# Down products of two feed-forward layers: seven block products in place of eight

## The chip, the core and the metric

The kernel runs on one core of one Trainium2 chip. The metric is the device time of one execution in microseconds (us). Matmuls run on TensorE (PE in the rows below, PEld for its weight loads), elementwise work on VectorE (DVE), ScalarE (ACT) and GpSimd (POOL); SyncE (SP) issues nearly all DMA transfers.

## The reference

Two transformer blocks over 1024 tokens of width 1024, in float32. Three feed-forward layers are in them, each with a hidden width of 2816 = 22 tiles of 128. The first has a convolution behind its up product; the second and third, which the change touches, are

```python
def swiglu(x, w_gu, w_down):
    g, u = jnp.split(x @ w_gu, 2, axis=-1)
    return (jax.nn.silu(g) * u) @ w_down

f = swiglu(rms_norm_2(h, ffn1_pre_g[i]), ffn1_w_gu[i], ffn1_w_down[i])
h = h + 0.5 * rms_norm_2(f, ffn1_post_g[i])
```

The order in the whole program: modulation, mixers and attention of block 1; feed-forward layer 1; layer 2; attention of block 2; layer 3; a gated embedding at the end.

## The kernel before

Every float32 operand of a matmul is split into a high and a low part (`Core.split`, lines 56 to 59: ACT copies the high part at line 58, DVE subtracts it at line 59), and each product is three matmuls: high by high, high by low, low by high. All matmuls of interest are 128 x 128 by 128 x 512.

`ffn` (line 189 on) has two stages.

**Up product.** Hidden tiles 0 and 1 are made plainly (lines 248 to 252). For tiles 2 to 21 the loop at line 323 makes gate and value together by seven block products (B11, T4, B21, T1, T2, B22, T3; `prod`, line 293: 12 matmuls each, 84 for one tile). `weights(j)` (line 271) loads the weights of one tile into `raw` buffers, makes differences on POOL and splits them. `finish_tile` (line 301) makes the gated hidden tile `s` and writes it to the DRAM tensor `hidden` (line 320). One pass of the loop takes five buffers of tag `b4`: T and t4 (lines 276 and 287), X (326), s and V (331).

**Down product.** `yacc` holds the eight output tiles of 128 tokens in SBUF. `load(j)` (line 355) brings back hidden tile j and the same 128 rows of `w_down` and splits both. `down` (line 366) takes a pair of hidden tiles and adds its product to `yacc`: for each of 8 token tiles and 2 column halves, 2 x 3 matmuls into one PSUM bank, then one add by DVE (line 377; ACT copies for the first pair, line 375). That is nine pairs of 96 matmuls, and at the end one call with four tiles (192 matmuls), between which the next norm is begun (`finish`).

Buffers: `b4` 12 of 4 KB per partition, `raw` 3, `wh` and `wl` 4 each, `hh` and `hl` 2 each of 16 KB (they hold the transposed input of the up product), PSUM `mm` 6 banks and `tp` 2. The tile framework decides the order on each engine: by the order of the program, but what is ready may go ahead of an earlier line that is not. A buffer is free again when all that reads it is done.

Of the kernel before, what the change touches and what calls it, by code (L numbers as in the profile page):

```python
# [5 lines left out]
F32 = mybir.dt.float32  # L6
F32R = mybir.dt.float32r
I32 = mybir.dt.int32
AF = mybir.ActivationFunctionType
OP = mybir.AluOpType  # L10
PSUM = bass.MemoryType.PSUM
DRAM = bass.MemoryType.DRAM
P = 128
D = 1024
# [174 lines left out]
def ffn(k, hT, w_gu, w_down, nff, prep, finish, taps=None, then=None):  # L189
# [2 lines left out]

    nc, v, pool = k.nc, k.nc.vector, k.nc.gpsimd
    with k.tc.tile_pool(name="ffn", bufs=1) as fp:
        k.places(fp, "b4", 12)
        hidden = k.dr.tile([nff, P, D], F32, name=f"hidden{k.count()}")

        def b4(dt=F32):  # L200
            return fp.tile([P, D], dt, name="b4", tag="b4", bufs=12)

        def big(shape, dt):
            return fp.tile([P] + shape, dt, name="S", tag="S", bufs=3)
# [54 lines left out]
        for a in range(0, 4, 2):  # L259
            c = slice(a, a + 2)  # L260
# [10 lines left out]
        def weights(j):  # L271

            rg, rv = k.raw([P, 8, P]), k.raw([P, 8, P])
            nc.sync.dma_start(rg, w_gu[:, j * P:j * P + P].rearrange("(k p) n -> p k n", p=P))
            nc.sync.dma_start(rv, w_gu[:, (j + nff) * P:(j + nff) * P + P].rearrange("(k p) n -> p k n", p=P))
            T = b4().rearrange("p (k n) -> p k n", k=8)
            pool.tensor_tensor(T[:, up], rv[:, up], rg[:, up], op=OP.subtract)
            W1 = [w.rearrange("p (k n) -> p k n", k=8) for w in k.wide()]
            k.split(*W1, rg)
            pool.tensor_tensor(T[:, dn], rv[:, dn], T[:, up], op=OP.subtract)  # L280
            pool.tensor_tensor(rv[:, up], rv[:, dn], rv[:, up], op=OP.subtract)
            W2 = [w.rearrange("p (k n) -> p k n", k=8) for w in k.wide()]
            k.split(*W2, T)
            W3 = [w.rearrange("p (k n) -> p k n", k=8) for w in k.wide()]
            k.split(*W3, rv)
            pool.tensor_tensor(T[:, up], rg[:, dn], T[:, dn], op=OP.subtract)  # L286
            t4 = b4(F32R).rearrange("p (a k n) -> p a k n", a=2, k=4)
            k.split(t4[:, 0], t4[:, 1], T[:, up])
            both = lambda W, c: (W[0][:, c], W[1][:, c])
            return dict(B11=both(W1, up), B21=both(W1, dn), T1=both(W2, up), T2=both(W2, dn), T3=both(W3, up),  # L290
                        B22=both(W3, dn), T4=(t4[:, 0], t4[:, 1]))

        def prod(ps, w, x, start):
            for a in range(4):
                for n, (y, z) in enumerate(((0, 0), (0, 1), (1, 0))):
                    nc.tensor.matmul(ps, w[y][:, a], x[z][:, a], start=start and a == 0 and n == 0, stop=a == 3 and n == 2,  # L296
                                     skip_group_check=True)

        lo, hi = slice(0, 512), slice(512, 1024)

        def finish_tile(j, A, w, s, V):

            prod(A, w["T4"], A22, False)
            if taps is None:
                nc.scalar.activation(s[:, hi], A, AF.Silu)
                v.tensor_tensor(s[:, hi], s[:, hi], V[:, hi], op=OP.mult)
            else:
                nc.scalar.activation(s[:, hi], A, AF.Copy)
                us = []
                for m, z in ((j, s), (j + nff, V)):  # L310
                    u = b4()
                    t = [taps[:, a, m:m + 1] for a in range(4)]
                    nc.scalar.activation(u, z, AF.Identity, bias=t[3], scale=t[1])
                    v.scalar_tensor_tensor(u[:, 1:], z[:, :D - 1], t[0], u[:, 1:], op0=OP.mult, op1=OP.add)
                    v.scalar_tensor_tensor(u[:, :D - 1], z[:, 1:], t[2], u[:, :D - 1], op0=OP.mult, op1=OP.add)
                    us.append(u)
                s = us[0]
                nc.scalar.activation(s, s, AF.Gelu_apprx_tanh)
                v.tensor_tensor(s, s, us[1], op=OP.mult)
            nc.sync.dma_start(hidden[j], s)  # L320

        prev = None
        for j in range(2, nff):
            w = weights(j)
            A, B, C = k.mm(), None, None
            X = b4()
            prod(A, w["B11"], A11, True)
            nc.scalar.activation(X[:, lo], A, AF.Copy)  # L328
            if prev is not None:
                finish_tile(*prev)  # L330
            s, V = b4(), b4()
            B = k.mm()
            prod(B, w["B21"], A12, True)
            v.tensor_tensor(s[:, lo], B, X[:, lo], op=OP.add)
            if taps is None:
                nc.scalar.activation(s[:, lo], s[:, lo], AF.Silu)
            C = k.mm()
            prod(C, w["T1"], S1, True)
            nc.scalar.activation(X[:, hi], C, AF.Copy)
            prod(A, w["T2"], S2, False)  # L340
            nc.scalar.activation(X[:, lo], A, AF.Copy)
            prod(C, w["B22"], S4, False)
            v.tensor_tensor(V[:, lo], C, X[:, lo], op=OP.add)  # L343
            if taps is None:
                v.tensor_tensor(s[:, lo], s[:, lo], V[:, lo], op=OP.mult)
            prod(A, w["T3"], S3, False)
            v.tensor_tensor(V[:, hi], A, X[:, hi], op=OP.add)
            prev = (j, A, w, s, V)
        finish_tile(*prev)


        ys = [big([4, D], F32) for _ in range(2)]
        yacc = [ys[i // 4][:, i % 4] for i in range(NT)]

        def load(j):
            r = k.raw([P, D])
            nc.sync.dma_start(r, hidden[j])
            h = b4(F32R), b4(F32R)
            k.split(*h, r)
            r = k.raw([P, D])  # L360
            nc.sync.dma_start(r, w_down[j * P:(j + 1) * P, :])
            w = k.wide()
            k.split(*w, r)
            return h + w

        def down(ready, first, last):
            for i in range(NT):
                t = slice(i * P, i * P + P)
                for n in range(2):
                    c = slice(n * 512, n * 512 + 512)  # L370
                    po = k.mm()
                    for a, (hh, hl, wh, wl) in enumerate(ready):
                        k.mm3(po, (hh[:, t], hl[:, t]), (wh[:, c], wl[:, c]), a == 0, a == len(ready) - 1)
                    if first:
                        nc.scalar.activation(yacc[i][:, c], po, AF.Copy)
                    else:
                        v.tensor_tensor(yacc[i][:, c], yacc[i][:, c], po, op=OP.add)  # L377
                if last:
                    finish(fp, i, yacc[i])
                    if i >= 4:  # L380
                        k.flush(2, 1)

        n = nff - 4
        for j in range(0, n, 2):
            down([load(j), load(j + 1)], j == 0, False)
        rows = big([4, D], F32)
        k.rows = [rows[:, a] for a in range(3)]
        k.junk = rows[:, 3]
        prep(fp)
        down([load(j) for j in range(n, nff)], False, True)  # L390
        k.close()
        if then is not None:
            then(fp)
# [10 lines left out]
class Filler:  # L404
# [21 lines left out]
    def finish(self, gen=None):  # L426
        while self.jobs and (gen is None or gen in self.jobs):
            self.step()
# [1299 lines left out]
def body(tc, ctx, p, out):  # L1728
# [80 lines left out]
    rows = []  # L1809
    fin, nxt2 = step(2, rows)  # L1810
    ffn(k, nxt[0], p["w_up"], p["w_down"], 22, loader(rows, (m[3], 1.0), (p["ffn1_pre_g_2"], 1.0)), fin, taps=taps)
    rows = []
    fin, nxt3 = step(3, rows)
    ffn(k, nxt2[0], p["ffn1_w_gu_2"], p["ffn1_w_down_2"], 22, loader(rows, (p["ffn1_post_g_2"], 0.5), (p["attn_pre_g_2"], 1.0)), fin)
    e = [k.dr.tile([P, D], F32, name=f"e{i}") for i in range(NT)]
    mT = attention2(k, nxt3[0], p["w_in_2"], p["b_in_2"], tabA, tabB, p["sinks_2"],
# [10 lines left out]
    def last(pool):  # L1827
        ple(k, pool, nxt5[0], e, p["w_ple_gate_2"], loader(rows6, (p["ple_post_g_2"], 1.0)), fin6)

    ffn(k, nxt4[0], p["ffn2_w_gu_2"], p["ffn2_w_down_2"], 22, loader(rows, (p["ffn2_post_g_2"], 0.5), (p["ple_pre_g_2"], 1.0)), fin,  # L1830
        then=last)

# [36 lines left out]
```

## Time and profile before

| | us |
|---|---|
| median of 3 runs | 3281.38 |
| lowest, highest | 3278.68, 3285.41 |
| the profiled execution | 3276.33 |
| its span, first to last instruction | 3274.3 |

The profile is that of one execution. The busy time of an engine is the time in which it runs instructions; matmuls overlap in their pipeline, so their mean duration is longer than the distance from one to the next. "Idle before" names what the engine waited for.

### The profile page before, as it was taken

How to read it: one execution, taken by the hardware profiler on the slowest of the kernel's cores; microseconds unless marked ns; L12 is line 12 of the kernel's file. 1: busy time of each engine (PE TensorE's matmuls, PEld its weight loads, DVE VectorE, ACT ScalarE, POOL GpSimd, SP SyncE). 2: the span in 40 equal slices, each digit the busy share in tenths (PEclk: the TensorE clock that was granted, in tenths of full speed). 3: DMA queues.
4: the chain of work that ended last, by engine and by line, in shares of the span. 5: the costliest groups of instructions: out<-in, count | busy, mean ns of one | idle time of the engine just before them, and what ended most of it. 6: DMA issues, size and time to landing. Idle time of an engine off the chain costs nothing. (4 is left out here: it accounts for less than half of the span.)

```text
span 3274.3 us, 40844 instructions
## 1 busy us (share of the span) xinstructions
PE 3088.8 (94%) x15362; PEld 2523.1 (77%) x15362; DVE 2133.0 (65%) x3648; ACT 1274.7 (39%) x1975; POOL 788.9 (24%) x903
## 2 busy tenths in 40 slices
PE   5989988899999998999999999999998999999988
PEld 2766767788887878888888878777787788888867
DVE  7766588766666678444446686667677444456686
ACT  3335633444543124333341145446623333341132
POOL 3468525322220014322300020000014222200022
PEclk8999999999999999999999999999998999999999
DMA  7573553122224232222242342111631222242344
GB/s 207 172 223 118 159 175 118 65 90 78 84 90 142 92 129 71 89 78 86 88 141 92 96 142 82 46 45 68 212 129 52 84 77 90 84 148 94 98 144 154
DMA packets 282104, 362.87 MB, mean 111 GB/s; under 512 B 35559, under 2 KB 208871, under 8 KB 281906
## 3 DMA queue, kind: packets, MB, share of 16 engines
q1 hardware_dynamic: 273442, 345.73, 32.7%
q10 hardware_dynamic: 6576, 9.00, 0.8%
q0 software_dynamic: 1888, 5.53, 0.6%
q8 instruction: 121, 1.98, 0.2%
q14 instruction: 77, 0.63, 0.1%
HBM read 274.84 MB, written 91.66 MB: 112 GB/s over the span
## 5 line engine op out<-in xcount | busy, mean ns | idle before, releaser
L296 PE MATMUL mm<-S,wh 128*128 128x512 f32 x1440 | 443.5, 389 | 2.0 <-ACT b L328 2.0
L96 PE MATMUL mm<-wh,b 128*128 128x512 f32 x1056 | 414.3, 393 | 4.0 <-ACT b L58 4.0
L97 PE MATMUL mm<-wl,b 128*128 128x512 f32 x1056 | 413.4, 392 | 0.0
L98 PE MATMUL mm<-wh,b 128*128 128x512 f32 x1056 | 411.9, 391 | 0.0
L377 DVE TENSOR_TENSOR S<-S,mm 128x512 f32<-128x512 f32 x432 | 289.1, 684 | 128.9 <-PE mm L98 128.0
L59 DVE TENSOR_TENSOR wl<-raw,wh 128x1024 fp32r<-128x1024 f32 x242 | 320.3, 1325 | 60.6 <-ACT wh L58 60.4
L58 ACT ACTIVATE wh<-raw 128x1024 fp32r<-128x1024 f32 x244 | 253.4, 1053 | 261.7 <-PE mm L296 140.2
L296 PEld LDWEIGHTS mm<-S,wh 128*128 128x128 f32 x1440 | 270.2, 188 | 58.6 <-ACT b L328 2.4
L96 PE MATMUL mm<-hh,wh 128*128 128x256 f32 (+1 forms) x880 | 300.1, 341 | 15.5 <-ACT hh L58 15.3
L97 PE MATMUL mm<-hl,wh 128*128 128x256 f32 (+1 forms) x880 | 298.9, 340 | 3.5 <-DVE hl L59 3.5
L98 PE MATMUL mm<-hh,wl 128*128 128x256 f32 (+1 forms) x880 | 297.0, 338 | 4.6 <-DVE wl L59 4.6
L296 PE MATMUL mm<-hh,wh 128*128 128x512 f32 x720 | 284.0, 395 | 13.6 <-ACT wh L58 9.8
L296 PE MATMUL mm<-hh,wl 128*128 128x512 f32 x720 | 283.5, 394 | 9.8 <-DVE wl L59 9.8
L296 PE MATMUL mm<-hl,wh 128*128 128x512 f32 x720 | 283.1, 393 | 0.0
L296 PE MATMUL mm<-S,wl 128*128 128x512 f32 x720 | 280.2, 389 | 0.0
L151 POOL TENSOR_TENSOR S<-S 128x1024 f32<-128x1024 f32 x24 | 58.9, 2453 | 802.6 <-ACT S L145 785.9
L343 DVE TENSOR_TENSOR b<-mm,b 128x512 f32<-128x512 f32 x60 | 41.5, 692 | 319.4 <-PE mm L296 314.1
L96 PEld LDWEIGHTS mm<-wh,b 128*128 128x128 f32 x1056 | 199.9, 189 | 45.6 <-ACT b L58 4.5
L97 PEld LDWEIGHTS mm<-wl,b 128*128 128x128 f32 x1056 | 200.0, 189 | 42.5 <-DVE wl L59 0.9
L98 PEld LDWEIGHTS mm<-wh,b 128*128 128x128 f32 x1056 | 199.2, 189 | 42.7 <-DVE b L59 1.2
L58 ACT ACTIVATE b<-raw 128x1024 fp32r<-128x1024 f32 x66 | 69.6, 1059 | 402.1 <-PE mm L97 247.6
L286 POOL TENSOR_TENSOR b<-raw,b 128x512 f32<-128x512 f32 x60 | 79.7, 1329 | 573.8 <-DVE wl L59 573.8
(385 smaller groups left out, 6454.0 us busy)
## 6 DMA issues: line engine op xcount, KB each, us to landing
raw<-in_ffn_w_gu SPq DMA_DIRECT2D x88, 512.0 KB, 3.8
hidden<-b SPq DMA_DIRECT2D x66, 512.0 KB, 2.6
raw<-hidden SPq DMA_DIRECT2D x66, 512.0 KB, 4.5
raw<-in_w_ada SPq DMA_DIRECT2D x48, 512.0 KB, 3.7
raw<-in_w_up SPq DMA_DIRECT2D x44, 512.0 KB, 3.8
raw<-in_ffn_w_down SPq DMA_DIRECT2D x44, 512.0 KB, 4.3
x<-tmp SPq DMA_DIRECT2D x40, 512.0 KB, 2.6
tmp<-x SPq DMA_DIRECT2D x40, 512.0 KB, 5.5
```

What stands on the lines that cost most here:

```text
L58: self.nc.scalar.activation(hi, src, AF.Copy)
L59: (eng or self.nc.vector).tensor_tensor(lo, src, f(hi), op=OP.subtract)
L96: mm(out, a[0], b[0], start=start, stop=False)
L97: mm(out, a[0], b[1], start=False, stop=False)
L98: mm(out, a[1], b[0], start=False, stop=stop)
L151: self.nc.gpsimd.tensor_tensor(y, y, row, op=OP.mult)
L286: pool.tensor_tensor(T[:, up], rg[:, dn], T[:, dn], op=OP.subtract)
L296: nc.tensor.matmul(ps, w[y][:, a], x[z][:, a], start=start and a == 0 and n == 0, stop=a == 3 and n == 2, skip_group_check=True)
L343: v.tensor_tensor(V[:, lo], C, X[:, lo], op=OP.add)
L377: v.tensor_tensor(yacc[i][:, c], yacc[i][:, c], po, op=OP.add)
```

## The change

It applies to the layers without convolution (`taps is None`). The hidden tiles 2 to 19 form nine pairs (p, p+1). The down product of a pair is a 2 x 2 block product: tokens in two halves (`lo`, `hi`: 512 tokens each), the pair's two tiles as the inner blocks, output columns in two halves. Seven block products replace the eight, with four sums of hidden blocks and four of weight blocks.

- During the up product, `weight_sums(p)` loads the two row blocks of `w_down`, makes four 128 x 512 differences on DVE and writes two tiles to the DRAM tensor `wsum`; it stands in pass p+2 of the loop, behind product T2. `hidden_sums(p)` makes four sums in place in the two `s` tiles, which are now kept, and writes two tiles to `hsum`; it stands in pass p+3.
- The down product runs over two groups, of four and of five pairs. For each of the seven names, `blocks()` loads one 128 x 512 hidden block and one weight block for every pair of the group (two DMAs of 256 KB), splits them into one `hh` and one `hl` buffer (a fifth pair into `wh`, `wl`), and `chain` runs four PSUM banks, with 4 x 3 or 5 x 3 matmuls in each, and evicts each bank into `yacc`. The loads and splits of a name stand one chain ahead in the program.
- Hidden tiles 0, 1, 20 and 21 go through the last plain call with four tiles, as tiles 18 to 21 did before.

```diff
+    pairs = list(range(2, nff - 2, 2)) if taps is None else []
...
+        def hidden_sums(j):
+
+            a, b = made.pop(j), made.pop(j + 1)
+            for o, x, y, op in ((b[:, hi], a[:, hi], b[:, hi], OP.add), (a[:, hi], a[:, lo], a[:, hi], OP.subtract),
+                                (a[:, lo], b[:, hi], a[:, lo], OP.subtract), (b[:, lo], b[:, lo], a[:, lo], OP.subtract)):
+                v.tensor_tensor(o, x, y, op=op)
+            nc.sync.dma_start(hsum[j - 2], a)
+            nc.sync.dma_start(hsum[j - 1], b)
+
+        def weight_sums(j):
+
+            a, b = b4(), b4()
+            nc.sync.dma_start(a, w_down[j * P:(j + 1) * P, :])
+            nc.sync.dma_start(b, w_down[(j + 1) * P:(j + 2) * P, :])
+            for o, x, y in ((a[:, lo], a[:, hi], a[:, lo]), (a[:, hi], b[:, hi], a[:, hi]),
+                            (b[:, hi], b[:, hi], a[:, lo]), (b[:, lo], b[:, lo], b[:, hi])):
+                v.tensor_tensor(o, x, y, op=OP.subtract)
+            nc.sync.dma_start(wsum[j - 2], a)
+            nc.sync.dma_start(wsum[j - 1], b)
...
             nc.scalar.activation(X[:, lo], A, AF.Copy)
+            if j - 2 in pairs:
+                weight_sums(j - 2)
+            if j - 3 in pairs:
+                hidden_sums(j - 3)
             prod(C, w["B22"], S4, False)
...
+        def blocks():
+
+            for js in groups:
+                for name in (1, 2, 5, 3, 6, 7, 4):
+                    H = k.g.tile([P, 4, D], F32R, name="hh", tag="hh", bufs=2)
+                    L = k.g.tile([P, 4, D], F32R, name="hl", tag="hl", bufs=2)
+                    r = []
+                    for m, j in enumerate(js):
+                        x = k.raw([P, D]) if m == 0 else b4()
+                        for c, src in zip((lo, hi), sources(name, j)):
+                            nc.sync.dma_start(x[:, c], src)
+                        h, l = (H[:, m], L[:, m]) if m < 4 else k.wide()
+                        k.split(h, l, x)
+                        r.append(((h[:, lo], l[:, lo]), (h[:, hi], l[:, hi])))
+                    yield r
...
+            def chain(banks, h, c, start, new):
+                ops = next(ahead)
+                for i, po in enumerate(banks):
+                    t = slice(i * P, i * P + P)
+                    for m, (x, y) in enumerate(ops):
+                        for z, (a, b) in enumerate(((0, 0), (0, 1), (1, 0))):
+                            nc.tensor.matmul(po, x[a][:, t], y[b], start=start and m == 0 and z == 0,
+                                             stop=m == len(ops) - 1 and z == 2, skip_group_check=True)
+                    y = yacc[i + 4 * h][:, c]
+                    if first and new:
+                        nc.scalar.activation(y, po, AF.Copy)
+                    else:
+                        v.tensor_tensor(y, y, po, op=OP.add)
...
+            U = [k.mm() for _ in range(4)]
+            chain(U, 0, lo, True, True)
+            chain(others(), 0, lo, True, False)
+            C = others()
+            chain(C, 1, hi, True, True)
+            chain(C, 0, hi, False, True)
+            chain(U, 0, hi, False, False)
+            chain(U, 1, hi, False, False)
+            chain(U, 1, lo, False, True)
+
+        groups = [pairs[:len(pairs) // 2], pairs[len(pairs) // 2:]] if pairs else []
...
+        plain = [j for j in range(nff) if j - j % 2 not in pairs]
+        n = len(plain) - 4
         for j in range(0, n, 2):
-            down([load(j), load(j + 1)], j == 0, False)
+            down([load(j) for j in plain[j:j + 2]], j == 0, False)
...
-        down([load(j) for j in range(n, nff)], False, True)
+        down([load(j) for j in plain[n:]], False, True)
```

`others()` gives two `mm` and two `tp` banks.

## Rows read from the trace of the kernel before

**Rows 1.** The page: busy time (share) of the engines, and granted clock in 40 slices.
```profile
PE 3088.8 (94%) x15362; PEld 2523.1 (77%) x15362; DVE 2133.0 (65%) x3648; ACT 1274.7 (39%) x1975; POOL 788.9 (24%) x903
...
PEclk8999999999999999999999999999998999999999
```
**Rows 2.** Busy time by stretch: up, down of layer 2; up, down of layer 3.
```profile
core 0: us, PE busy (x) PEld busy (x) DVE busy (x) ACT busy (x) POOL busy (x), PEclk, DMA share, GB/s
1300.00:1640.00 340.00, 337.86 (x1476) 278.85 (x1476) 153.60 (x164) 119.46 (x163) 100.87 (x72) 0.99 0.27 86
1700.00:1860.00 160.00, 160.00 (x707) 132.53 (x706) 106.75 (x142) 32.87 (x38) 0.00 (x0) 1.00 0.32 102
2526.00:2870.00 344.00, 341.01 (x1496) 282.02 (x1497) 154.18 (x165) 121.39 (x165) 99.57 (x72) 0.99 0.26 85
2908.00:3085.00 177.00, 177.00 (x781) 146.28 (x780) 115.81 (x151) 42.68 (x51) 0.00 (x0) 1.00 0.36 116
```
**Rows 3.** Timeline of PE in the down product: start, duration, engine, line.
```profile
1700.03 0.39 PE L96 MATMUL mm<-wh,b 128*128 128x512 f32 x1
...
1702.75 0.39 PE L96 MATMUL mm<-wh,b 128*128 128x512 f32 x1
```
**Rows 4.** Groups by line in the down product, 1700 to 1860: busy, mean ns.
```profile
L377 DVE TENSOR_TENSOR S<-S,mm 128x512 f32<-128x512 f32 x111 | 74.2, 684 | 36.2 <-PE mm L98 36.0
...
L59 DVE TENSOR_TENSOR b<-raw,b 128x1024 fp32r<-128x1024 f32 x15 | 18.3, 1223 | 15.3 <-ACT b L58 15.3
...
L58 ACT ACTIVATE b<-raw 128x1024 fp32r<-128x1024 f32 x15 | 15.9, 1061 | 123.7 <-PE mm L97 83.1 <-DMA raw<-hidden 40.6
```
**Rows 5.** Timeline of DVE in the up product, one pass and the next's start.
```profile
1444.26 0.69 DVE L334 TENSOR_TENSOR b<-mm,b 128x512 f32<-128x512 f32 x1 [1.04 <-PE mm L296]
1452.49 0.69 DVE L343 TENSOR_TENSOR b<-mm,b 128x512 f32<-128x512 f32 x1 [7.54 <-PE mm L296]
1453.21 0.69 DVE L345 TENSOR_TENSOR b<-b,b 128x512 f32<-128x512 f32 x1
1453.83 1.22 DVE L59 TENSOR_TENSOR wl<-b,wh 128x1024 fp32r<-128x1024 f32 x1
1455.14 0.69 DVE L347 TENSOR_TENSOR b<-mm,b 128x512 f32<-128x512 f32 x1
1455.75 1.75 DVE L59 TENSOR_TENSOR wl<-raw,wh 128x1024 fp32r<-128x1024 f32 x1
1457.42 0.68 DVE L59 TENSOR_TENSOR b<-b,b 128x512 fp32r<-128x512 f32 x1
1458.02 1.21 DVE L59 TENSOR_TENSOR wl<-raw,wh 128x1024 fp32r<-128x1024 f32 x1
1461.21 0.99 DVE L306 TENSOR_TENSOR b<-b,b 128x512 f32<-128x512 f32 x1 [1.98 <-ACT b L305]
1463.30 0.69 DVE L334 TENSOR_TENSOR b<-mm,b 128x512 f32<-128x512 f32 x1 [1.10 <-PE mm L296]
```
**Rows 6.** Line 306 alone: count, duration min/median/max in ns.
```profile
L306 DVE TENSOR_TENSOR b<-b,b x40: 684/1000/1427, 1327.9 to 2914.8; 128x512 f32<-128x512 f32 x40
```
**Rows 7.** Timelines of PE, ACT, POOL, SP in the same pass, where buffers change hands.
```profile
1441.11 0.39 PE L296 MATMUL mm<-hh,b 128*128 128x512 f32 x1
1456.45 0.63 ACT L58 ACTIVATE b<-b 128x512 fp32r<-128x512 f32 x1 [0.47 <-POOL b L286]
1457.86 0.60 ACT L328 ACTIVATE b<-mm 128x512 f32<-128x512 f32 x1 [0.78 <-PE mm L296]
1460.37 1.29 POOL L277 TENSOR_TENSOR b<-raw 128x512 f32<-128x512 f32 x1 [3.95 <-DMA raw<-in_ffn_w_gu]
1476.47 0.68 DVE L59 TENSOR_TENSOR b<-b,b 128x512 fp32r<-128x512 f32 x1
1462.23 0.34 SPq L320 DMA_DIRECT2D hidden<-b  x1
```
**Rows 8.** DMA issues of the page: KB each, median us from issue to landing.
```profile
hidden<-b SPq DMA_DIRECT2D x66, 512.0 KB, 2.6
...
raw<-in_ffn_w_down SPq DMA_DIRECT2D x44, 512.0 KB, 4.3
```
**Rows 9.** DMA between 2320 and 2340 us: rate in 40 slices, packets.
```profile
GB/s 397 410 389 377 455 385 205 217 258 283 373 360 381 410 430 401 139 0 33 0 0 16 0 94 111 389 401 401 389 410 401 426 365 410 418 410 397 406 414 406
DMA packets 2745, 6.08 MB, mean 304 GB/s; under 512 B 165, under 2 KB 173, under 8 KB 2743
...
q1 hardware_dynamic: 2743, 6.06, 85.1%
```
**Rows 10.** Timeline of PE where layer 2 goes from up to down.
```profile
1683.19 0.39 PE L296 MATMUL mm<-S,wl 128*128 128x512 f32 x1
1683.42 0.39 PE L96 MATMUL mm<-wh,b 128*128 128x512 f32 x1
...
1685.28 0.39 PE L97 MATMUL mm<-wl,b 128*128 128x512 f32 x1
1685.51 0.40 PE L296 MATMUL mm<-hh,b 128*128 128x512 f32 x1
```

More of the change, by code (lines that the diff above doesn't have):

```diff
@@ L198, in ffn @@
         hidden = k.dr.tile([nff, P, D], F32, name=f"hidden{k.count()}")
+        if pairs:
+            hsum = k.dr.tile([2 * len(pairs), P, D], F32, name=f"hsum{k.count()}")
+            wsum = k.dr.tile([2 * len(pairs), P, D], F32, name=f"wsum{k.count()}")
         def b4(dt=F32):
@@ L320, in finish_tile @@
             nc.sync.dma_start(hidden[j], s)
+            if pairs:
+                made[j] = s
+        made = {}
+        def hidden_sums(j):
[14 more added lines that the diff above has]
+            nc.sync.dma_start(wsum[j - 1], b)
         prev = None
@@ L381, in down, with sources @@
                         k.flush(2, 1)
-        n = nff - 4
+        def sources(name, j):
+            row = lambda x: w_down[x * P:(x + 1) * P]
+            p = j - 2
+            return {1: (hidden[j][:, lo], row(j)[:, lo]), 2: (hidden[j + 1][:, lo], row(j + 1)[:, lo]),
+                    3: (hsum[p + 1][:, lo], row(j + 1)[:, hi]), 4: (hidden[j + 1][:, hi], wsum[p + 1][:, lo]),
+                    5: (hsum[p + 1][:, hi], wsum[p][:, lo]), 6: (hsum[p][:, lo], wsum[p + 1][:, hi]),
+                    7: (hsum[p][:, hi], wsum[p][:, hi])}[name]
@@ new lines, in group, with others @@
+        def group(first):
+            def chain(banks, h, c, start, new):
[11 more added lines that the diff above has]
+                        v.tensor_tensor(y, y, po, op=OP.add)
+            def others():
+                return [k.mm() for _ in range(2)] + [
+                    k.ps.tile([P, 4, P], F32, name="tp", tag="tp", bufs=2).rearrange("p a b -> p (a b)") for _ in range(2)]
+            U = [k.mm() for _ in range(4)]
[7 more added lines that the diff above has]
+            chain(U, 1, lo, False, True)
@@ L384, in ffn, with one_ahead @@
+        groups = [pairs[:len(pairs) // 2], pairs[len(pairs) // 2:]] if pairs else []
+        if pairs:
+            def one_ahead(g):
+                was = next(g)
+                for x in g:
+                    yield was
+                    was = x
+                yield was
+            ahead = one_ahead(blocks())
+            for a in range(2):
+                group(a == 0)
+        plain = [j for j in range(nff) if j - j % 2 not in pairs]
+        n = len(plain) - 4
         for j in range(0, n, 2):
-            down([load(j), load(j + 1)], j == 0, False)
+            down([load(j) for j in plain[j:j + 2]], j == 0, False)
```

## The prediction

> **What bounds the kernel now.** I read the page first: PE is busy 94% of the span, DVE 65%, ACT 39%, at a granted clock of nine tenths or more in nearly every slice [rows 1]. Shares over the whole span mix stages, so the next view is busy time by stretch, for the two stages that the change touches. In the down product of layer 2 PE is busy 160.00 of 160.00 us, in layer 3 177.00 of 177.00; in the up products 337.86 of 340.00 and 341.01 of 344.00; the clock is 0.99 to 1.00, its upper level [rows 2]. DVE has slack everywhere: 153.6 of 340 us in the up stretch, 106.75 of 160 in the down stretch. POOL does nothing in the down product, and DMA runs at about a third of its share. So PE sets both stages, and what a matmul costs is the distance from one to the next, not its 0.39 us: from 1700.03 to 1702.75 twelve matmuls start, 2.72 / 12 = 0.2267 us each [rows 3]. One pass of the up loop is 84 matmuls = 19.04 us, just the distance of line 334 from itself (1444.26 to 1463.30) [rows 5].
>
> **The change, part by part.**
>
> *Removed.* Before, one layer's down product has 22 tiles x 16 banks x 3 = 1056 matmuls. After: 9 pairs x 7 products x 4 banks x 3 = 756, and 4 plain tiles x 48 = 192, together 948. 108 fewer, of the same shape, in each of two layers: 216 x 0.2267 = 49.0 us, all of it on the engine that sets the end.
>
> The Trainium skill ("TensorE: Matmul & The Clock Gate", Back-to-back issue gap) gives 131 ns for a 512-column matmul in a sustained stream of weight loads and matmuls. Rows 3 disagree: 226.7 ns. By the page's figure the same 216 matmuls would be worth 28 us; the measured distance decides.
>
> *Down product, the handover of operand buffers.* This is the part that can eat the gain. Blocks are split into two `hh`/`hl` buffers, so the splits of chain n+1 can start only when chain n-1 has ended, and must be done within chain n: 48 matmuls = 10.9 us in the first group, 60 = 13.6 us in the second. The work: first ACT copy 1.06 us, then four DVE subtractions of 1.22 [rows 4], behind one add of 0.68 left from the chain before: 1.06 + 4 x 1.22 + 0.68 = 6.6 us, some 7 with the hand-overs between engines. The fifth pair goes through its own buffers, and adds 1.2 us. 7 < 10.9 and 8.2 < 13.6: cover of 4 to 5 us. If the cover is gone, PE waits for the difference, 28 times. DVE also has four bank adds of 0.684 in a chain: 4.9 + 2.7 = 7.6 of 10.9 us, 8.8 of 13.6. Bank reuse: a chain starts on a bank that was finished a chain earlier; three of its adds can come behind the splits, by about 9.1 us, before the first bank is wanted at 10.9. I take 0; bounds 0 and 1 us for each of 28 chains, 28 us.
>
> *Down product, DMA.* A chain moves 512 KB for each pair: 4 x 524,288 B / 10.88 us = 193 GB/s, where the stretch has 102 to 116 now [rows 2]. Rows of the transfers become 2 KB long. Between 2320 and 2340 us packets of 6.08 MB / 2745 = 2.2 KB mean ran at 360 to 430 GB/s for many slices, on the same queue [rows 9]. So half of what was shown is needed, and `b4` and `raw` let loads run two to three chains ahead: 0.
>
> *Up product, DVE.* Each pair adds 8 operations of 128 x 512, both inputs in SBUF. The same form at line 306 takes 684 ns at best, 1000 median, 1427 at most [rows 6]: 5.5 to 11.4 us for two passes, in which DVE idles 2 x (19.04 - 153.6 x 19.04/340) = 20.9 us. Each pass has one hole of 7.54 us, ahead of line 343 [rows 5]; four operations (2.7 to 5.7 us) fit into it. What stands behind them in DVE's queue is line 343 and the splits for the next tile. PE wants those late: the T1 and T2 weights, whose split ends at 1455.05 [rows 5], are used when B21 of the next pass ends, which is what line 334 at 1463.30 waits for. So DVE may slip 8 us before PE notices. The weight sums wait for their loads, 4.3 us [rows 8]; even if DVE sat through the whole landing, 4.3 + 2.7 stays under 8. Taken as 0; bounds 0 and 1 us for each of 18 pairs, 18 us.
>
> The Trainium skill ("SBUF — State Buffer", Who interferes with whom) speaks against this part: a DVE operation with two SBUF inputs and a GpSimd operation that reads SBUF exclude each other, and the loser waits. Rows 6 agree, with up to 1427 ns instead of 684. At that maximum all 144 new operations cost 206 us of DVE time, still inside the idle time above.
>
> *Up product, SP and DMA.* Two loads and four writes of 512 KB more for each pair, 3.1 MB in 38 us = 83 GB/s, on top of 86 [rows 2]: under half of rows 9. SP issues in order: a sum's write that waits for DVE holds back the `w_gu` loads behind it. POOL starts on such a load as soon as it lands (its idle time ends on that DMA), but DVE's split of that T comes 12 us later (1460.37, and 1453.83 + 19.04) [rows 5, 7]. 0.
>
> *Up product, `b4` buffers.* Now alive, one pass each: T from POOL's start at 1460.37 to 1477.15, 16.8 us; t4 from 1456.45 to its last matmul, 1441.11 two passes later, 22.7; X 17.0 (line 328 to the end of line 347 a pass later); s from 1444.26 to its landing at 1462.23 + 2.6, 20.6; V 9.7 [rows 5, 7, 8]. 86.8 / 19.04 = 4.6 buffers of 12 on average. The sums keep s of the first tile 24 to 50 us longer, that of the second 5 to 31 (early or late in the queue), and two weight tiles about 12 us each: (31 to 81 + 24) / 38.08 = 1.4 to 2.8 more. 6.0 to 7.4 of 12: enough on average, with the peak near 10 to 12.
>
> *Joints.* At the end of the up product PE fills the wait for the last T4 with 8 matmuls of the down product, 1683.42 to 1685.51 [rows 10]. The first chain now needs an input buffer that is free only after B21 of the last tile, five products or 13.6 us before the end. Its splits take 6 to 7 us beside DVE's last evictions and the last hidden sum (2.7). If it comes in time, 0; if not, these 2.1 us are bare and some 4 more of splits follow. I take 2 us a layer, 4 in all; bounds 0 and 12. The last four plain tiles are as before: 0.
>
> *Sum:* -49.0 + 4 = -45 us. Against the profiled execution: 3276.33 - 45 = 3231.3. The median of the runs is 5.05 us above that execution, so 3281.4 - 45 = 3236.
>
> **Rivals.**
>
> 1. *Short cover.* The handover takes longer than a chain (splits queue behind bank adds, loads land late), or the up passes lose up to 1 us a pair: 28 + 18 + 8 more at the joints is the upper end, so 3240 to 3280; about 3255. For it: splits rise from 44 to 71 a layer. Against it: 4 us of cover in each chain.
>
> 2. *Slower: the sums starve `b4`.* Two passes draw exactly 12 `b4` tiles (5 + 5 + 2) and there are 12. If s of tile p+2 can have its buffer only when `hsum` of pair p has landed, and DVE takes `hidden_sums` at its place in the program, in pass p+3 behind T2, then s comes at 19.04 + 13.6 + 2.7 + 2.6 = 38 us of its pass instead of 8.2 us (behind B11, T4, B21), 29.7 late. PSUM covers one pass (six `mm` banks, three a tile), so PE stands 29.7 - 19.0 = 10.7 us in each of 18 pairs: 190 us, about 3422. It decides from 49 / 18 = 2.7 us a pair on. For it: the peak above. Against it: instructions do go ahead of earlier lines (the split at 1453.83 stands in the program behind line 347, at 1455.14) [rows 5], so the sums can use the hole a pass earlier; and any free buffer may serve.
>
> 3. *It does nothing:* losses of 42 to 55 us from a mixture of the bounds: 3281. That the matmuls are fewer but PE's time is not would need a PE that waits now; it does not [rows 2].
>
> **How the numbers follow.** A measurement of this kernel can tell about 0.2% (6.6 us) from no change. Forecast, 3228 to 3246: 0.66. Short cover, 3246 to 3274: 0.16. No difference: 0.05. Slower: 0.13. Faster 0.82, same 0.05, slower 0.13. The range: 3281.4 - 49 with 4 us of scatter below, 3228, up to 3266, which takes in the forecast and most of the short-cover case.
>
> **What would show it.** PE with 216 matmuls fewer, about 215 us for the down product of each layer instead of 239; PE busy over 99% in both stages; 0.2267 us from matmul to matmul; DMA near 190 GB/s in the down stretch; up passes still 19.04 us apart. Wrong would be: waits of PE on line 58 or 59 once in each chain (rival 1), or up passes longer than 19.04 with X, s or V waiting for a buffer (rival 2).

## The result and the profile after

The changed kernel took 3233.14 us (median of 4 runs, 3229.38 to 3238.82) against 3282.75 us; the ratio is 0.9851, 95% interval 0.9833 to 0.9870. A later set of runs of the same kernel (`after_again` below) took 3230.39 us, ratio 0.9844 (0.9830 to 0.9859) to the kernel before on the same chip. The gain is 49.6 us by the first pair of medians, 51.7 us by the second. The forecast was 3236 us, between 3228 and 3266.

The page of the changed kernel, the line that answers to [rows 1]:

```profile
PE 3046.4 (94%) x15146; PEld 2485.3 (77%) x15146; DVE 2180.7 (67%) x3670; ACT 1325.2 (41%) x2029; POOL 790.3 (24%) x903
```

PE has 15362 - 15146 = 216 matmuls fewer, and 42.4 us less busy time; DVE and ACT have some 50 us more each. The share of PE is unchanged at 94%, so this line does not say where the time went. The views by stretch do. Busy time of the changed kernel: a piece of layer 2's up product, the down product of layer 2, the up product of layer 3, the down product of layer 3 (columns as in [rows 2]):

```profile
1500.00:1600.00 100.00, 100.00 (x443) 82.84 (x442) 61.88 (x74) 35.30 (x48) 28.61 (x21) 1.00 0.50 176
1690.00:1865.00 175.00, 175.00 (x772) 144.37 (x771) 106.88 (x112) 75.63 (x85) 0.00 (x0) 1.00 0.65 221
2516.00:2890.00 374.00, 371.25 (x1638) 307.20 (x1637) 215.41 (x250) 129.35 (x177) 105.31 (x76) 1.00 0.47 162
2892.00:3066.00 174.00, 174.00 (x768) 143.48 (x767) 106.80 (x112) 75.75 (x86) 0.00 (x0) 1.00 0.64 222
```

PE is busy in every microsecond of both down stretches, and 175.00 / 772 = 0.2267 us is the distance from matmul to matmul, as in [rows 3]. In the up products DVE went from 45% (153.6 of 340 us, [rows 2]) to 62% in the piece of layer 2 and 58% in layer 3, ACT and POOL stayed, DMA doubled from 86 to 162 or 176 GB/s, and PE lost nothing (2.75 us idle in layer 3's stretch, 2.99 us before).

By landmarks of the two traces: from the first matmul of the down product to the last, layer 2 took 251.1 us before (1683.4 to 1934.5) and 225.7 after (1690.6 to 1916.3); from the start of layer 3's down product to the end of the span it was 365.6 and is 340.5. That is 25.4 and 25.1 us, with 24.5 forecast for each from the matmul count alone. The up loop of layer 3, from the first to the last matmul whose operand is a sum of inputs (`S`), took 375.5 and takes 375.2 us. The two profiled spans differ by 41.4 us only, because 4.5 us are longer ahead of layer 2's loop and 1.9 us between layer 2's down and layer 3's up, where the change does nothing, and 2.6 in layer 2's loop (373.4 us before, 376.0 after). The 2.6 us do not come from the sums: the loop takes 373.3 us in the trace of `after_again`, and 373.6 us in that of the run with the sums alone. The medians of several runs, with 50 us, are the better measure.

**The sums in the up product.** Timeline of DVE in one pass of layer 2 after the change, which answers to [rows 5]:

```profile
1508.59 0.69 DVE L364 TENSOR_TENSOR b<-mm,b 128x512 f32<-128x512 f32 x1 [1.10 <-PE mm L302]
1510.53 0.69 DVE L337 TENSOR_TENSOR b<-b,b 128x512 f32<-128x512 f32 x1 [1.25 <-DMA hidden<-b]
1511.26 0.69 DVE L337 TENSOR_TENSOR b<-b 128x512 f32<-128x512 f32 x1
1511.98 0.69 DVE L337 TENSOR_TENSOR b<-b,b 128x512 f32<-128x512 f32 x1
1512.59 0.68 DVE L348 TENSOR_TENSOR b<-b 128x512 f32<-128x512 f32 x1
1513.19 0.68 DVE L337 TENSOR_TENSOR b<-b,b 128x512 f32<-128x512 f32 x1
1513.79 1.41 DVE L348 TENSOR_TENSOR b<-b,b 128x512 f32<-128x512 f32 x2
1515.24 0.69 DVE L348 TENSOR_TENSOR b<-b 128x512 f32<-128x512 f32 x1
1516.82 0.69 DVE L377 TENSOR_TENSOR b<-mm,b 128x512 f32<-128x512 f32 x1 [0.89 <-PE mm L302]
```

Lines 364 and 377 are lines 334 and 343 of the kernel before. All eight operations of a pair (337: hidden sums, 348: weight sums) lie between them, in the hole that was 7.54 us wide; 1.25 us of it are left ahead of them and 0.89 us behind. Their places in the program are later, and the two sets stand a pass apart; the hidden sums waited only for the write of `hidden` (1.25 us), and the weight sums followed among them.

**The handover of a buffer.** ACT and DVE in the middle of layer 2's down product (line 456 adds a bank to `yacc`):

```profile
1737.99 1.05 ACT L58 ACTIVATE hh<-raw 128x1024 fp32r<-128x1024 f32 x1
1738.94 2.94 ACT L58 ACTIVATE hh<-b 128x1024 fp32r<-128x1024 f32 x3
```
```profile
1739.07 1.23 DVE L59 TENSOR_TENSOR hl<-raw,hh 128x1024 fp32r<-128x1024 f32 x1 [6.25 <-ACT hh L58]
1740.21 3.49 DVE L59 TENSOR_TENSOR hl<-b,hh 128x1024 fp32r<-128x1024 f32 x3
1743.62 1.28 DVE L456 TENSOR_TENSOR S<-S,mm 128x512 f32<-128x512 f32 x2
```

From the first copy to the end of the fourth subtraction it is 1743.70 - 1737.99 = 5.7 us of a chain of 10.9. The bank adds come behind, as worked out, and PE waits for nothing in this stretch.

**The joint.** PE where layer 2 goes from up to down, which answers to [rows 10]:

```profile
1690.40 0.39 PE L302 MATMUL mm<-S,wl 128*128 128x512 f32 x1
1690.63 0.39 PE L450 MATMUL mm<-hh 128*128 128x512 f32 x1
1690.85 0.39 PE L450 MATMUL mm<-hl,hh 128*128 128x512 f32 x1
1691.08 0.39 PE L450 MATMUL mm<-hh,hl 128*128 128x512 f32 x1
1691.31 0.39 PE L450 MATMUL mm<-hh 128*128 128x512 f32 x1
1691.57 0.50 PE L302 MATMUL mm<-hh,b 128*128 128x512 f32 x1
```

The first pair of the first chain was split in time, and ACT had copied the high part of the second: three matmuls of the one and one of the other (line 450) are the filling ahead of the last T4. PE does not stop. The other pairs had to wait for their loads and not for the input buffer:

```profile
1688.64 1.06 ACT L58 ACTIVATE hh<-b 128x1024 fp32r<-128x1024 f32 x1 [2.60 <-DMA b<-in_ffn_w_down]
```

### The profile page after: what moved, and what is told of

Read it like the earlier page. It is cut to its first block, busy times and chain, and to the rows that moved or that the text cites. A ratio compares the mean times of both kernels' runs of the same rounds, so it can differ in the third digit from the quotient of the medians.

```text
span 3232.9 us, 40832 instructions
## 1 busy us (share of the span) xinstructions
PE 3046.4 (94%) x15146; PEld 2485.3 (77%) x15146; DVE 2180.7 (67%) x3670; ACT 1325.2 (41%) x2029; POOL 790.3 (24%) x903
## 5 line engine op out<-in xcount | busy, mean ns | idle before, releaser
L58 ACT ACTIVATE wh<-raw 128x1024 fp32r<-128x1024 f32 x208 | 217.4, 1055 | 263.2 <-PE mm L302 142.5
L59 DVE TENSOR_TENSOR wl<-raw,wh 128x1024 fp32r<-128x1024 f32 x206 | 277.2, 1347 | 41.0 <-ACT wh L58 40.7
L96 PEld LDWEIGHTS mm<-hh,wh 128*128 128x128 f32 x880 | 171.3, 195 | 33.7 <-ACT hh L58 16.9
L96 PE MATMUL mm<-wh,b 128*128 128x512 f32 x480 | 189.9, 397 | 4.0 <-ACT b L58 4.0
L97 PE MATMUL mm<-wl,b 128*128 128x512 f32 x480 | 189.2, 395 | 0.0
L98 PE MATMUL mm<-wh,b 128*128 128x512 f32 x480 | 187.4, 392 | 0.0
L98 PEld LDWEIGHTS mm<-hh,wl 128*128 128x128 f32 x880 | 170.9, 195 | 21.2 <-DVE wl L59 4.9
L97 PEld LDWEIGHTS mm<-hl,wh 128*128 128x128 f32 x880 | 171.5, 195 | 18.4 <-DVE hl L59 4.1
L151 POOL TENSOR_TENSOR tmp<-tmp,row 128x1024 f32<-128x1024 f32 x16 | 42.3, 2646 | 583.7 <-DMA raw<-in_ffn_w_gu 445.5
L302 PEld LDWEIGHTS mm<-hh,wh 128*128 128x128 f32 x720 | 137.3, 191 | 44.3 <-ACT wh L58 10.4
```

The source lines that it names most:

```text
L58: self.nc.scalar.activation(hi, src, AF.Copy)
L59: (eng or self.nc.vector).tensor_tensor(lo, src, f(hi), op=OP.subtract)
L96: mm(out, a[0], b[0], start=start, stop=False)
L97: mm(out, a[0], b[1], start=False, stop=False)
L98: mm(out, a[1], b[0], start=False, stop=stop)
L151: self.nc.gpsimd.tensor_tensor(y, y, row, op=OP.mult)
```

## The experiments

The theory: the whole gain is 216 matmuls at 0.2267 us, and everything added lies beside them. The rivals: the sums or their buffers cost the up product something, the handover costs the down product something, or part of the gain has another source.

### The sums alone

```diff
-        if pairs:
+        if False:
             def one_ahead(g):
...
-        plain = [j for j in range(nff) if j - j % 2 not in pairs]
+        plain = list(range(nff))
```

> The up side of the change alone: hidden_sums and weight_sums are made and written in both layers, but the down product is that of the kernel before (eight products, pairs of tiles), so hsum and wsum go unread. Theory (the sums lie in DVE's idle time and cost nothing): the time of the kernel before, 3281 us, between 0 and 3 us more. Rival (the sums lengthen the up passes by up to 1 us a pair, which the gain of the down product then hides): up to 18 us more, 3299. Rival (the kept tiles starve b4): 190 us more.

Measured: 3282.77 us against 3279.70 (19 runs) on that chip, ratio 1.0006 (0.9996 to 1.0015). The up product of layer 2 with the sums in it, and then the same stretch of the kernel before:

```profile
1320.00:1680.00 360.00, 360.00 (x1589) 297.83 (x1588) 204.91 (x244) 124.64 (x171) 99.63 (x73) 1.00 0.47 164
```
```profile
1320.00:1680.00 360.00, 360.00 (x1590) 298.09 (x1589) 158.52 (x171) 125.83 (x172) 99.58 (x73) 1.00 0.27 85
```

DVE has 46 us more, DMA twice the rate, PE 1589 matmuls in place of 1590. The interval reaches from -1 to 5 us, so a cost of a few us in both layers together is not excluded; the 18 us of the first rival and the 190 us of the second are out.

### An eighth product put back

```diff
...
-            chain(U, 1, lo, False, True)
+            ops = chain(U, 1, lo, False, True)
+            chain(others(), 0, lo, True, False, ops, False)
```

The last two arguments hand in the operands of the chain before and leave the evictions out; the lines of `chain` that make them possible are cut here.

> The changed kernel with an eighth chain in each group: the operands of the last chain once more into four spare banks that nobody reads, 48 + 60 = 108 matmuls a layer, the number that the change removed. No further DMA, split or bank add. Theory (the whole gain is matmuls at 0.2267 us): 216 x 0.2267 = 49 us more than the changed kernel, 3282, the time of the kernel before within 4 us. Rival (part of the gain is from the bank adds, 72 instead of 160 a layer, or from other work that went): stays clearly under the kernel before, 3233 to 3270.

Measured: 3281.04 us, ratio 1.0006 (0.9996 to 1.0015) to the kernel before: the gain is gone, within the interval of -1 to 5 us. The down product of layer 2 in this kernel:

```profile
1700.00:1860.00 160.00, 160.00 (x707) 132.53 (x706) 94.57 (x99) 67.89 (x76) 0.00 (x0) 1.00 0.60 207
```

Its DVE is busy 94.57 us where that of the kernel before was busy 106.75 [rows 2], and that is worth nothing. With the run before, this settles where the gain comes from: the sums cost nothing that can be measured, and the 216 matmuls account for all of the gain, to some 5 us.

### Every split made twice

```diff
                         k.split(h, l, x)
+                        k.split(h, l, x)
```

> The changed kernel with every split of a block made twice (ACT copy and DVE subtraction, same result), so the handover of a buffer costs double. Theory (7 us of work in a chain of 10.9 us, 8.2 in 13.6): doubled, DVE has 8 x 1.22 = 9.8 us of splits and 2.7 of bank adds for 10.9, or 12.2 + 2.7 for 13.6; over by 1.6 us in the three chains of the first group that DVE evicts, 0.2 in the four that ACT evicts, 1.3 in the seven of the second group: 15 us a layer, some 30 in all, 3263. If there is no cover at all, each added subtraction lies bare: 7 x 4.9 + 7 x 6.1 = 77 us a layer, 154 in all, 3387. If the cover is larger than worked out: 3233 to 3240.

Measured: 3248.02 us, ratio 0.9906 (0.9887 to 0.9926), 15 to 20 us above the changed kernel (by the medians and by the ratios), against the 30 worked out. The first stretch of layer 2's down product, the piece of it behind PE's wait, and the wait:

```profile
1690.00:1772.00 82.00, 78.45 (x332) 63.87 (x331) 75.63 (x74) 67.81 (x77) 0.00 (x0) 0.96 0.74 259
1718.40:1725.00 6.60, 6.57 (x16) 5.24 (x17) 6.60 (x8) 3.96 (x5) 0.00 (x0) 0.53 0.64 246
```
```profile
PE mm L451 <- DVE S L457: 3.4, 1, 3.4
```

DVE is now busy 92% of the first stretch, and PE waits 3.4 us for a bank add (line 457), once in the layer. Behind that wait the granted clock is 0.53 for 6.6 us, the lower of its two levels: 16 matmuls, where 29 fit at 0.2267 us, so another 3 us are lost. From the first to the last matmul of the chains a layer takes 180.9 and 181.6 us, where it takes 173.1 in `after_again`: 16 us more in the two together, about half of them waits. So 10 us of DVE splits in a chain nearly fit and the cover of the handover is there; without any cover it would have been 154 us.

### The changed kernel again, and shorter chains

> The changed kernel as it is, as the base for the other three on the same chip: 3233 us, ratio 0.985.

Measured: 3230.39 us, ratio 0.9844, the base for the next three.

```diff
-        groups = [pairs[:len(pairs) // 2], pairs[len(pairs) // 2:]] if pairs else []
+        groups = [pairs[a:b] for a, b in ((0, 2), (2, 4), (4, 6), (6, 9))] if pairs else []
...
-            for a in range(2):
+            for a in range(len(groups)):
```

> The changed kernel with four groups of 2, 2, 2 and 3 pairs in place of 4 and 5, so chains of 24 matmuls, 5.4 us; 112 bank adds or copies a layer instead of 56, the same matmuls, loads and splits. Theory (what must fit into a chain: 1.06 + 2 x 1.22 + 0.68 = 4.2 us of handover, and 2 x 1.22 + 4 x 0.684 = 5.2 us of DVE): both still fit, so 3233 to 3240. Rival (each handover costs PE something, up to 1 us a chain): 28 more chains than the changed kernel, up to 28 us more, 3261.

Measured: 3229.96 us, ratio 0.9848 (0.9831 to 0.9864): the same. Twice the chains and twice the bank adds cost nothing; DVE is busy 134.05 of 160 us, PE 160.00:

```profile
1700.00:1860.00 160.00, 160.00 (x708) 132.48 (x707) 134.05 (x159) 70.48 (x76) 0.00 (x0) 1.00 0.62 207
```

A cost of each handover of the size of the rival, 28 us in all, is ruled out. With nine groups of one pair (`[(a, a + 1) for a in range(9)]` in the first of these lines):

> Nine groups of one pair: chains of 12 matmuls, 2.72 us, 63 a layer. Theory (DVE becomes the bound): 1.22 of split and 4 x 0.684 of bank adds are 3.96 us a chain, 1.24 over, in the 56 chains that DVE evicts: 69 us a layer, 139 in all, 3372, slower than the kernel before. Rival (only the handover of a buffer counts, 1.06 + 1.22 + 0.68 + 0.3 = 3.3 us, 0.55 over in 63 chains): 70 us in all, 3303.

Measured: 3344.13 us, ratio 1.0191 (1.0175 to 1.0206), slower than the kernel before, and 114 us over the changed one, where 139 were worked out. The bound is the one named, DVE. Its timeline, and what PE waited for between 1700 and 1880:

```profile
1801.89 2.47 DVE L456 TENSOR_TENSOR S<-S,mm 128x512 f32<-128x512 f32 x4
1804.29 1.22 DVE L59 TENSOR_TENSOR hl<-raw,hh 128x1024 fp32r<-128x1024 f32 x1
1805.42 2.47 DVE L456 TENSOR_TENSOR S<-S,mm 128x512 f32<-128x512 f32 x4
1807.81 1.22 DVE L59 TENSOR_TENSOR hl<-raw,hh 128x1024 fp32r<-128x1024 f32 x1
```
```profile
PE mm L450 <- DVE S L456: 24.9, 22, 2.1
PE mm L450 <- ACT hh L58: 2.3, 2, 1.2
```

DVE has no gap. Its period is 1805.42 - 1801.89 = 3.53 us, not the 3.96 of the summed durations: back to back, an operation starts before the end of the one before, every 0.60 us for an add of 0.684 and 1.13 for a split of 1.22. DVE evicts 59 of the 63 chains of a layer (ACT four of the first group; the expectation counted 56), so the period gives (3.53 - 2.72) x 59 x 2 = 96 us. From the first to the last matmul of the chains the two layers take 223.1 and 222.2 us where they take 173.1 each in `after_again`, 99 us more. The rest of the 114 lies mainly in the plain call behind them (63.8 us in place of 52.5 in layer 2, 60.6 in place of 54.5 in layer 3).

In the run with doubled splits the same overlap makes 8 x 1.13 + 4 x 0.60 = 11.4 us for a chain of 10.9, less over than the 1.6 us worked out for each of three chains. Why PE then waits 3.4 us in one place was not traced.

### Fewer b4 buffers

```diff
+        held = [b4() for _ in range(4 if pairs else 0)]
+        for x in held:
+            v.memset(x, 0.0)
         prev = None
         for j in range(2, nff):
...
+        for x in held:
+            v.tensor_tensor(x[:, :1], x[:, :1], prev[4][:, D - 1:], op=OP.add)
         finish_tile(*prev)
```

> The changed kernel with four of the twelve b4 buffers held (written before the up loop, read at its end) in the two layers, so the up passes have eight. Theory (6 to 7.4 alive on average, and what would wait first is a weight load that nobody is in a hurry for): within 5 us of the changed kernel, 3233 to 3238. Rival (b4 is at its edge with twelve): 10 us or more, and PE waits behind X, s or V in the up passes.

Measured: 3238.89 us, ratio 0.9867 (0.9853 to 0.9882), 8.5 us over the base, between the two expectations. The trace puts it at the start of the up loops: there PE waits 11.5 us in layer 2 (7.1 of them once, for a weight split) and 9.1 in layer 3, where it waits 7.6 and 6.6 in `after_again`. In all the passes after that it waits for 0.2 us. With six held:

> As with four held b4 buffers, but six, so the up passes of layers 2 and 3 have six. Four held cost 8.5 us, and by the trace all of that ahead of the first pass (where the sums of the input take b4 tiles), none in the passes. Theory (the passes hold 5.2 tiles on average before the sums come in, 6 to 7.4 with them): six are too few, the passes stretch, 30 us or more over the changed kernel. Rival (what waits is never urgent): only the start gets longer, 10 to 20 us more.

Measured: 3236.15 us, ratio 0.9872 (0.9855 to 0.9888): no worse than four, as far as the intervals tell. The expectation of 30 us or more was wrong. The memsets of the held buffers, at the start of the two layers, and three stretches of layer 2's passes:

```profile
L354 DVE MEMSET b<- x12: 912/912/912, 1295.4 to 2506.5; 128x1024 f32 x12
```
```profile
1390.00:1490.00 100.00, 100.00 (x440) 82.29 (x440) 60.09 (x69) 34.09 (x47) 31.90 (x22) 1.00 0.49 170
1490.00:1590.00 100.00, 100.00 (x443) 82.82 (x442) 58.91 (x69) 33.36 (x45) 27.33 (x19) 1.00 0.48 164
1590.00:1680.00 90.00, 90.00 (x398) 74.18 (x396) 54.39 (x62) 32.49 (x45) 30.41 (x20) 1.00 0.48 166
```

Six buffers carry the passes, sums and all, at full speed. What is left is at the start, where each memset is 0.91 us of DVE in a stretch in which PE waits for DVE anyway; how much of the 6 to 9 us is the memsets and how much the missing buffers, these runs do not tell.

### The first layer too

```diff
-    pairs = list(range(2, nff - 2, 2)) if taps is None else []
+    pairs = list(range(2, nff - 2, 2))
```

> The change also in the first layer, whose up pass has a convolution: DVE is busy 253.7 of 380 us there (12.7 of each 19.04 us pass) and a pass takes seven b4 tiles, not five. Theory (only the matmul count decides as long as DVE has room): 108 x 0.2267 = 24.5 us less than the changed kernel, 3209. Rival (DVE's idle time in that layer lies in pieces of 4 us at most, and nine b4 tiles a pass on average are too many): the passes of layer 1 stretch, and 10 us or more of the 24.5 are lost.

Measured: 3214.25 us, ratio 0.9798 (0.9783 to 0.9813), and once more:

> The kernel with the change in all three layers once more, as the base on the same chip for the next one: ratio 0.980, some 3215 us.

3214.95 us, ratio 0.9807 (0.9793 to 0.9822). It beats both kernels, the one before by 63 to 65 us and the changed one by 15 to 19, but not by the 24.5 of the count. So 6 to 9 us are lost, less than the 10 or more of the rival, but in its way: the passes of layer 1 stretch. Layer 1's loop takes 384.3 us in `all_layers_again` (first to last S product) where it takes 374.6 in `after_again`, on the same chip; 24.5 - 9.7 = 14.8 us is about the gain measured there, 15.4. In the trace of `all_layers` PE waits for ACT's copy at line 371 eight times, which it does not in the changed kernel:

```profile
PE mm L302 <- ACT b L371: 7.3, 8, 1.0
```

One of these passes, and behind it the same place in the changed kernel:

```profile
743.47 0.60 ACT L314 ACTIVATE b<-mm 128x512 f32<-128x512 f32 x1 [1.69 <-PE mm L302]
744.68 3.38 DVE L337 TENSOR_TENSOR b<-b,b 128x512 f32<-128x512 f32 x2
747.99 3.50 DVE L320 SCALAR_TENSOR_TENSOR b<-b,taps,b 128x1023 f32<-128x1023 f32 x2
753.80 0.68 DVE L364 TENSOR_TENSOR b<-mm,b 128x512 f32<-128x512 f32 x1
755.23 0.74 PE L302 MATMUL mm<-S,wh 128*128 128x512 f32 x2 [0.92 <-ACT b L371]
```
```profile
760.05 0.60 ACT L314 ACTIVATE b<-mm 128x512 f32<-128x512 f32 x1 [2.12 <-PE mm L302]
761.96 3.34 DVE L320 SCALAR_TENSOR_TENSOR b<-b,taps,b 128x1023 f32<-128x1023 f32 x2 [3.79 <-ACT b L319]
767.61 0.68 DVE L364 TENSOR_TENSOR b<-mm,b 128x512 f32<-128x512 f32 x1
```

With the convolution (lines 320 and 321) in its queue DVE has no hole of 7.5 us. The last two hidden sums stand in front of the convolution, and line 364 comes 10.3 us behind ACT's line 314 instead of 7.6. ACT's copy at line 371 may not overwrite X before that add has read it (in both kernels it waits 0.7 us for it), and PE waits for the copy where it comes late. The two sums take 3.38 us here, 1.69 each, where the same operations take 0.69 in layer 2: in this pass GpSimd runs three operations between 744.45 and 749.21, and in the pass of layer 2 shown further up none while the sums run. How much of the loss is the slower sums and how much the lack of a hole was not separated.

The next run gives the sums of layer 1 to GpSimd, which is busy 104 of 380 us there in the changed kernel:

```diff
+        sumeng = v if taps is None else pool
...
-                v.tensor_tensor(o, x, y, op=op)
+                sumeng.tensor_tensor(o, x, y, op=op)
```

(and the same in `weight_sums`).

> As the one above, but the sums of layer 1 are made by GpSimd, not by DVE (layers 2 and 3 unchanged). Theory (with the sums in its queue DVE takes line 364 late in layer 1, ACT's line 371 waits for that and PE for ACT, 7.3 us in eight times; GpSimd has 380 - 104 us free there): those waits go, 5 to 7 us less, 3209. Rival (a GpSimd operation of this form takes 1.3 us or more, and it and DVE's two-input operations get in each other's way): no gain, or a loss.

Measured: 3227.95 us, ratio 0.9845 (0.9831 to 0.9860): 13 us worse, where 5 to 7 us of gain were expected. The waits grew, and GpSimd waits for loads of `w_down` with its own work behind (groups in 605 to 985 us; line 283 is line 277 of the kernel before):

```profile
PE mm L302 <- ACT b L372: 18.6, 8, 2.6
```
```profile
L338 POOL TENSOR_TENSOR b<-b,b 128x512 f32<-128x512 f32 x24 | 41.6, 1732 | 0.6
L283 POOL TENSOR_TENSOR b<-raw 128x512 f32<-128x512 f32 x19 | 38.3, 2015 | 48.4 <-DMA raw<-in_w_up 48.4
L349 POOL TENSOR_TENSOR b<-b 128x512 f32<-128x512 f32 x17 | 27.9, 1639 | 75.1 <-DMA b<-in_w_down 75.1
```

The weight sums (line 349) stand in GpSimd's queue in front of the differences that the next tile's weights wait for, and GpSimd stands 75.1 us for their loads. Its operations are slower too, though not all: line 283 takes 2.02 us on average instead of 1.40 in `all_layers_again`, line 286 takes 1.84 instead of 1.46, and line 287 takes 1.82 instead of 2.08. How much of the loss is the queue and how much the slower operations was not separated.

## Why the prediction was right

- **The size.** 49.0 us from the count and the distance; 49.6 and 51.7 by the medians, 25.4 and 25.1 a layer in the traces. The eighth product put back takes the gain away, to 5 us. This step was the forecast, and it held because PE waited for nothing in these stretches, before or after. The 215 and 239 us named as signs count matmuls alone; the landmarks, 225.7 and 251.1 us, also hold the last T4 and the waits of the last call, some 11 us on either side.
- **The joints** were mis-sized: 2 us a layer were added for the first chain's splits. One pair split in time was enough to fill the wait for T4, and PE does not stop in either layer: the term is about 0. Without it the forecast would have been 3232, and 3233.14 and 3230.39 were measured. The input buffer, of which the term was made, came free about when it was worked out (ACT's first copy starts at 1679.95, some 14 us before the last T4 ends); what was late was the loads.
- **DVE in the up product.** Four operations were placed in each pass's hole. All eight of a pair went into one hole of 7.54 us, at 0.69 us each, not at the 1.0 to 1.43 of line 306: GpSimd's operations fall outside this hole (none between 1509.89 and 1519.45 in the pass shown), while line 306 runs beside them in the passes looked at. Eight at 1.0 us would have been longer than the hole; that they meet no GpSimd operation there was not worked out ahead, and was luck. The cost of 0 was right (the run with the sums alone, to 5 us). In layer 1, where no such hole is left and some of the sums meet GpSimd, the same operations cost 7 to 10 us of loop time: so the hole, not DVE's busy share, was the right thing to argue from.
- **The handover.** 6.6 to 7 us of work in 10.9 were worked out; 5.7 us were seen. The cover was understated a little: no bank add stood ahead of the splits (0.68 us), and the four subtractions took 4.63 us where the sum of their durations is 4.88.
- **`b4`.** The average of 6.0 to 7.4 of 12 was no guide to what is needed: six are enough. The rival of 190 us had its chance of 0.13 from a fixed order of the sums, which the trace shows to be wrong; the argument against it (work that is ready goes ahead) was the better one and deserved more weight. Two slips in the working change nothing: 24 + 5 is 29 and not 31 for the hidden tiles, and rival 1's losses, 28 + 18 + 8 us on top of 3236, end at 3290 and not at 3280.
- **DMA.** 193 GB/s were forecast for the down stretch and 221 came: the loads of the last four plain tiles, 8 x 512 KB or 24 GB/s over the 175 us, fall into the same stretch and were left out, as were some of the next stage. It changed nothing, at 0.65 of the DMA share.

## What to carry to other kernels

Where PE has no idle time in a stretch, matmuls taken away are worth their distance from start to start, and the question is only whether the added work fits into real holes of the other engines, in their order of issue. A hole as long as the moved work, with its inputs ready ahead of it, is evidence; a busy share below one is not (in layer 1 DVE was idle 33% of the time, and the sums still cost time). Moving the work to an engine with more idle time can be worse: here its queue stood for the loads of the added work, with work behind it that others waited for.

## What the runs showed that was not expected

DVE's operations overlap when they stand back to back: adds of 0.684 us start every 0.60 us, splits of 1.22 us every 1.13 us, so sums of durations overstate a full DVE by about a tenth. A sum of two SBUF tiles of 128 x 512 took 0.69 us in layer 2 and up to 1.69 in layer 1, where GpSimd ran at the same time. And six `b4` buffers in place of twelve leave the up passes at full speed, sums included.
